# A retention loop with its score product one projection later and its value product one tile later, and its input loads a tile ahead

## The chip, the cores and the metric

The kernel runs on one core of one Trainium2 chip. A core has a matrix engine (TensorE, in the profile PE, with its weight loads as PEld) and three others that work beside it: VectorE (DVE), ScalarE (ACT) and GpSimd (POOL). SyncE (SP) issues most DMAs, and ACT a few. Each engine takes its own instructions in the order in which they stand in its queue. The metric is the device time of one execution, in microseconds (us); lower is better.

## The reference

One decoder layer on 2048 tokens of width 1024, in float32:

```python
h = x * (1.0 + scale_m) + shift_m                  # modulation from a conditioning vector
z = h @ w_in                                       # columns: 3 x 512 for a short convolution,
                                                   # 4 x 512 for q, k, v, g of 4 retention heads of 128
q = rotary(q); k = rotary(k) * 128 ** -0.5
# retention in chunks of 128 tokens (a "tile"), with a state carried from chunk to chunk
scores = einsum('bnihd,bnjhd->bhnij', qc, kc) * decay_mask
intra  = einsum('bhnij,bnjhe->bnihe', scores, vc)
inter  = einsum('bnihd,hi,nbhde->bnihe', qc, xi, prev_states)
y_ret  = silu(g) * head_groupnorm(intra + inter)
mix    = concat([y_conv, y_ret]) @ w_out
x = layernorm(alpha * x + gate_m * mix)
x = layernorm(alpha * x + gate_f * swiglu(x * (1 + scale_f) + shift_f))
```

## The kernel before

Each float32 matrix product is made of three float16 products (`mm3`, lines 135 to 137): both operands are split into a high and a low half (`split`, ACT at line 130 writes the high half, DVE at line 131 the low one). A program schedules the instructions of each engine from the written order, so some stand a little away from where they are written; the change section shows where they stand.

The stage of this case is a loop over the 128-token tiles t = 4 to 15 of the retention group. What one tile does:

- `gemm_ret(t, u)` for u = 0 to 3 projects the tile to k, q, v and g: 24 matmuls each into a PSUM bank, then one eviction, for u = 0 on DVE (L705), for u = 1 and 2 on ACT (L709), for u = 3 on ACT with silu (L711).
- `rotary(t)`: three DVE products (L734 to L736), then two POOL sums (L737, L738).
- `ret_transpose(t - 1)`: splits the rotated q and k of the tile before (ACT L130, DVE L131), sends each half through a transposing DMA on SP (L753), and lets POOL add the two halves of q (L756).
- `ret_scores(t - 1)`: 12 short float16 matmuls on the transposed q and k, evicted by DVE with the decay mask (L767).
- `ret_kv(t - 1)`: 4 float32 matmuls (L776) for the state; DVE adds (L782), POOL decays (L784).
- `ret_y(t - 1)`: 8 float32 matmuls (L793 with the scores, L796 with the state), then per-head statistics on DVE (L800, L802), the root on POOL (L804, L805), gate times root on POOL (L807), and the normalised product on DVE (L810). `ret_part` splits the result and frees the tile's pages; `ret_mix` stores it by a transposing DMA (L832).

Beside this the loop prepares later tiles. A pair of tiles shares one 256-token block of the input. `xt_load` brings a block from HBM (L231), `ret_h` modulates it on ACT (L296), `ret_hsplit` splits it, and `h_more` makes sums on POOL (L344 to L347), splits those too and stores all for the convolution (L356). In the tiles 7, 10, 11 and 13 an earlier block is loaded and treated again (`h_again`). The scale of all blocks from the fifth on comes from `h_scale()` in tile 6: DVE finds a bound (its last step is L291) and one small matmul (L99) spreads it over the partitions.

Memory is 24 pages of 8 KB per partition. `page(at)` takes a page from the list of free ones: with `at=0` the one freed longest ago, with `at=1` the next. A load into a page waits on SP until the last reader of that page is done, and everything behind it on SP waits too.

After the loop come the convolution group, the output projection with the first layer norm, the SwiGLU layer in two halves, and the second layer norm.

Of the kernel before, what the change touches and what calls it, by code (L numbers as in the profile page):

```python
# [24 lines left out]
NT = T // P  # L25
# [15 lines left out]
def kernel(ctx: ExitStack, tc: tile.TileContext, xT, x, c, adaN, adaT, ada_b, w_ret, w_conv,  # L41
# [187 lines left out]
    def xt_load(p, at=0):  # L229
        pg = page(at=at)  # L230
        nc.sync.dma_start(pg, xT[p])  # L231
        xt_pg[p] = pg
# [458 lines left out]
    def gemm_ret(t, u):  # L691
        hv, i4, _, ivh = hr[t // 2]
        if t not in qp:
            qp[t] = page(at=1)
        w_hi, w_lo = ret_w[u]
        ps = bank()
        for k in range(KT):
            mm3(ps, hv[:, t % 2, k // 4, 0, k % 4], hv[:, t % 2, k // 4, 1, k % 4], w_hi[:, k], w_lo[:, k],
                k == 0, k == KT - 1)
        dst = qp[t][:, u * 512:(u + 1) * 512]  # L700
        iv = i4[:, u:u + 1]
        if t % 2 == 0:
            nc.gpsimd.tensor_mul(iv, ivw[:, u:u + 1], ivh)
        if u == 0:
            nc.vector.scalar_tensor_tensor(  # L705
                dst.rearrange("p (h n) -> p h n", h=HEADS), ps.rearrange("p (h n) -> p h n", h=HEADS), iv,
                cst[:, 4:8][:, :, None].to_broadcast([P, HEADS, P]), op0=OP.mult, op1=OP.mult)
        elif u != 3:
            nc.scalar.activation(dst, ps, AF.Copy, scale=iv)  # L709
        else:  # L710
            nc.scalar.activation(dst, ps, AF.Silu, scale=iv)  # L711
# [46 lines left out]
    def ret_scores(t):  # L758
        tt = T1[t]
        th = tt.bitcast(F16)  # L760
        ps = aux()
        for h in range(HEADS):
            v = slice(h * P, (h + 1) * P)
            o = h * P
            mm3(ps[:, v], th[:, o:o + P], th[:, 1024 + o:1152 + o], th[:, 512 + o:640 + o], th[:, 1536 + o:1664 + o],
                True, True)
        nc.vector.scalar_tensor_tensor(tt[:, 1024:1536].rearrange("p (h n) -> p h n", h=HEADS),  # L767
                                       ps.rearrange("p (h n) -> p h n", h=HEADS), qk_s[t // 2][1],
                                       mask[:, None, :].to_broadcast([P, HEADS, P]), op0=OP.mult, op1=OP.mult)
# [47 lines left out]
    def ret_part(t):  # L817
        r = T1[t][:, 1536:2048]
        s = col(1, "s")
        row_scale(RM.pop(t), s, ivr[:, t:t + 1])  # L820
        rr = t2k(F16)
        split(r, rr[:, :512], rr[:, 512:1024], s)
        RR[t] = rr
        free(qp.pop(t), T1.pop(t))
# [35 lines left out]
    def cw_max(u):  # L860
        unit_max(cw_stage[u])
# [50 lines left out]
    def last_modulation():  # L912
        ada_bias(40, 48)
        row_of(mod[:, 5 * KT:6 * KT], gfrow, 1.0 / ALPHA)
# [160 lines left out]
    AGAIN = (7, 10, 11, 13)  # L1075
    for t in range(4, NT):
        p = t // 2 + 1
        if t % 2 == 0 and p < 8:
            xt_load(p, 1)
        end = t == NT - 1  # L1080
        ret_transpose(t - 1)
        gemm_ret(t, 0)
        if end:
            free(*ret_pages[0:2])
            cw_load(1)
            cw_max(0)
        if 4 < t < 13:
            ada_sum(t + 3)
        gemm_ret(t, 1)
        if 3 < t < 12:  # L1090
            ada_load(t + 4, -1)
        if end:
            free(*ret_pages[2:4])
            cw_split(0)
            cw_max(1)
            hp_load(0, 0)
            hp_load(0, 5)
        ret_scores(t - 1)
        ret_kv(t - 1)
        rotary(t)  # L1100
        if t == 4:
            ret_xmax(p)
        if t in (4, 5):
            for i in range(2):
                x_scan(2 * t - 4 + i)
        if t == 6:
            h_scale()
        if t in AGAIN:
            xt_load(AGAIN.index(t), 1)
        gemm_ret(t, 2)  # L1110
        if t > 4:
            ret_mix(t - 2)
        if end:
            free(ropep, *ret_pages[4:6])
            hp_load(0, 4)
            hp_load(0, 1)
            hp_load(0, 6)
        if t % 2 == 0 and p < 8:
            ret_h(p)
            ret_hsplit(p)  # L1120
        if t == NT - 2:
            cw_load(0)
        gemm_ret(t, 3)
        ret_y(t - 1)
        ret_part(t - 1)
        if end:
            free(*ret_pages[6:8])
            hp_load(0, 3)
            hp_load(0, 2)
        if t == 4:  # L1130
            ret_mix(2)
        if t in AGAIN:
            h_again(AGAIN.index(t))
        elif chores:
            chores.pop()()
        if t % 2 == 1:
            free(hr.pop(t // 2)[2])
# [31 lines left out]
    for b in range(2):  # L1169
        for u in range(6):  # L1170
            n = 6 * b + u
            if n == 5:
                for _ in range(3):
                    hp_load(1, ahead.pop(0))
            if n < 5:
                cw_split(u + 1)
                if u < 4:
                    cw_load(u + 2)
                    cw_max(u + 2)
            elif n < 11:  # L1180
                cw_again((u + 1) % 6)

            def done(m, b=b, u=u):
                if u == 5:
                    free(hp.pop((b, m)))
                    if b == 0 and ahead:
                        hp_load(1, ahead.pop(0))

            if 4 <= n < 8:
                ada_load(12 + n, -1)  # L1190
                ada_load(16 + n, -1)
            if 5 <= n < 9:
                ada_sum(11 + n)
                ada_sum_both(15 + n)
            if n == 3:
                mix_modulation()
            if n == 8:
                free(crow)
            if n == 9:
                more_modulation()  # L1200
            if n == 11:
                last_modulation()
            if n == 1:
                ret_scores(NT - 1)
                ret_mix(NT - 2)
            if n == 2:
                ret_y(NT - 1)
                free(spp)
            conv_pair(u, b, done)
            if n == 0:  # L1210
                ret_transpose(NT - 1)
            if n == 2:
                ret_part(NT - 1)
            if n == 3:
                ret_mix(NT - 1)
            if n == 6:
                conv_mix(0)
            if n == 7:
                wo_load(0)
            if n == 8:  # L1220
                wo_max(0)
                wo_split(0)
                wo_load(1)
            if n == 4:
                free(*cw_tmp)
            if n == 9:
                wo_max(1)
                wo_split(1)
                mixr_load(0)
            if n == 11:  # L1230
                mixr_load(2)
                mixr_load(1)
# [661 lines left out]
```

## Time and profile before

| | us |
|---|---|
| three runs | 2122.60, 2124.27, 2130.06 |
| median | 2124.27 |
| the profiled execution, device time | 2129.92 |
| its span in the trace | 2128.1 |
| PE busy | 2026.9 (95%) |
| DVE busy | 1461.7 (69%) |
| POOL busy | 953.9 (45%) |
| ACT busy | 666.7 (31%) |

The span lies 1.8 us below the device time of the same execution. PE is the engine that is busy nearly always, so a gain has to come out of the time in which it waits or runs at the lower of its two clocks. The core's mean granted clock was 0.987 of full speed.

### The profile page before, as it was taken

What the parts mean: (1) busy time and instruction counts of PE and PEld (TensorE: products, weight loads), DVE (VectorE), ACT (ScalarE), POOL (GpSimd) and SP (SyncE); (2) the same over time, 40 slices, a digit from 0 to 9 for tenths busy, and PEclk for the clock granted to TensorE, in tenths of its full rate; (3) what the DMA queues carried; (4) which work ended last, traced back from release to release, by engine and by line L of the source; (5) the groups of instructions that cost most, each with busy time, mean ns of one, the idle gap of its engine ahead of it and who ended that gap; (6) DMA issues with size and microseconds to landing.
All of it is one profiled execution on the core that took longest, in us unless ns stands there. A gap on an engine that the chain in (4) does not pass through costs nothing.

```text
span 2128.1 us, 24625 instructions
## 1 busy us (share of the span) xinstructions
PE 2026.9 (95%) x9631; PEld 949.7 (45%) x9631; DVE 1461.7 (69%) x1769; ACT 666.7 (31%) x728; POOL 953.9 (45%) x759
## 2 busy tenths in 40 slices
PE   8899898989899999799999999999999899999998
PEld 4355444444444544344444444444444344444443
DVE  7899556667677577768745677777767454378564
ACT  5522443424322222323323233333432122122210
POOL 3554655555742277733312344444447333134232
PEclk9999999999999999999999999999999999999999
DMA  9047454586684288765411234343345874475311
GB/s 375 25 136 237 129 159 109 150 263 190 219 315 168 82 236 200 176 180 205 149 50 60 98 131 144 126 141 134 135 167 203 298 309 175 157 271 189 149 71 78
DMA packets 189492, 361.06 MB, mean 170 GB/s; under 512 B 118080, under 2 KB 118080, under 8 KB 166592
## 3 DMA queue, kind: packets, MB, share of 16 engines
q1 hardware_dynamic: 181168, 344.55, 48.3%
q10 hardware_dynamic: 8208, 14.95, 2.0%
q8 instruction: 75, 1.23, 0.2%
q14 instruction: 41, 0.34, 0.0%
HBM read 231.26 MB, written 100.93 MB: 156 GB/s over the span
## 4 chain that ended last, share of the span: by engine, by line
PE 47%; DVE 5%; POOL 4%; DMA 4%; issue 2%; ACT 1%; SPq 0%; POOLq 0%; DVEq 0%; ACTq 0%
PE ax L135 8%; PE ax L136 8%; PE ax L137 8%; PE mm L135 8%; PE mm L136 8%; PE mm L137 8%; DMA pg<-in_w_dn_dram 1%; POOL pg L1612 1%; DMA pg<-yscr 1%; DMA yscr<-pg 1%; DVE wdm L87 1%; ACT pg L1272 1%; DVE pg L1611 1%; DVE pg L1335 1%; POOL pg L1336 1%
## 5 line engine op out<-in xcount | busy, mean ns | idle before, releaser
L135 PE MATMUL mm<-pg,pg 128*128 128x512 f16 x1604 | 608.6, 381 | 23.2 <-ACT pg L1420 8.2
L136 PE MATMUL mm<-pg,pg 128*128 128x512 f16 x1604 | 611.1, 381 | 0.0
L137 PE MATMUL mm<-pg,pg 128*128 128x512 f16 x1604 | 610.2, 381 | 0.5 <-DVE pg L889 0.5
L135 PE MATMUL ax<-pg,pg 128*128 128x512 f16 x1220 | 463.1, 380 | 12.4 <-DVE pg L1301 2.9
L136 PE MATMUL ax<-pg,pg 128*128 128x512 f16 x1220 | 463.2, 380 | 0.0
L137 PE MATMUL ax<-pg,pg 128*128 128x512 f16 x1220 | 461.6, 380 | 0.6 <-DVE pg L889 0.6
L135 PEld LDWEIGHTS <-pg 128*128 128x128 f16 x2888 | 284.1, 98 | 362.9 <-DMA pg<-pg 16.0
L136 PEld LDWEIGHTS <-pg 128*128 128x128 f16 x2888 | 284.1, 98 | 356.1 <-issue 30.4
L137 PEld LDWEIGHTS <-pg 128*128 128x128 f16 x2888 | 283.9, 98 | 350.3 <-issue 18.8
L1470 POOL TENSOR_TENSOR pg<-pg,t2k 128x512 f32<-128x512 f32 x44 | 57.9, 1317 | 328.6 <-DVE x L114 194.0
L131 DVE SCALAR_TENSOR_TENSOR pg<-pg,p2s,pg 128x2048 f16<-128x2048 f32 (+1 forms) x42 | 92.7, 2216 | 138.1 <-ACT pg L130 138.0
L130 ACT ACTIVATE pg<-pg,p2s 128x2048 f16<-128x2048 f32 (+1 forms) x42 | 77.5, 1858 | 262.3 <-PE mm L136 114.1
L1407 DVE TENSOR_TENSOR pg<-pg,pg 128x2048 f16<-128x2048 f32 x22 | 50.3, 2286 | 69.8 <-ACT pg L1406 69.8
L87 DVE TENSOR_REDUCE m<-pg 128x2 bf16<-128x2048 f32 (+1 forms) x38 | 86.3, 2276 | 16.2 <-DMA pg<-in_w_gu_dram 10.0
L525 PE MATMUL mm<-pg,pg 128*128 128x512 f16 x384 | 91.1, 393 | 5.6 <-DVE pg L533 2.5
L1475 ACT ACTIVATE pg<-t2k,ivg 128x512 f32<-128x512 f32 x44 | 31.5, 716 | 174.3 <-DVE t2k L1474 174.3
L1523 ACT ACTIVATE pg<-pg 128x2048 f16<-128x2048 f32 (+1 forms) x22 | 37.3, 1697 | 107.8 <-DMA wscr<-pg 69.6
L1524 DVE TENSOR_TENSOR pg<-pg,pg 128x2048 f16<-128x2048 f32 (+1 forms) x22 | 44.4, 2016 | 38.8 <-ACT pg L1523 38.8
L131 DVE SCALAR_TENSOR_TENSOR pg<-pg,hs,pg 128x1024 f16<-128x1024 f32 x32 | 48.5, 1535 | 29.2 <-ACT pg L130 29.0
L1264 POOL TENSOR_SCALAR rs<-mv 128x1 f32<-128x1 f32 x32 | 30.5, 957 | 82.2 <-DVE mv L1262 79.6
L1577 POOL TENSOR_TENSOR pg<-pg,pg 128x2048 f32<-128x2048 f32 (+1 forms) x6 | 26.9, 4490 | 82.0 <-DVE pg L131 38.6
L525 PEld LDWEIGHTS <-pg 128*128 128x128 f16 x384 | 38.0, 101 | 53.8 <-issue 10.0
(278 smaller groups left out, 2834.6 us busy)
## 6 DMA issues: line engine op xcount, KB each, us to landing
pg<-wscr SPq DMA_DIRECT2D x28, 1024.0 KB, 5.0
pg<-in_w_gu_dram SPq DMA_DIRECT2D x22, 1024.0 KB, 4.8
uscr<-pg SPq DMA_DIRECT2D x44, 512.0 KB, 2.7
pg<-in_w_dn_dram SPq DMA_DIRECT2D x22, 1024.0 KB, 5.8
pg<-in_adaT_dram SPq DMA_DIRECT2D x21, 1024.0 KB, 7.2
wscr<-pg SPq DMA_DIRECT2D x77, 256.0 KB, 2.9
yscr<-pg SPq DMA_DIRECT2D x16, 1024.0 KB, 4.9
pg<-uscr SPq DMA_DIRECT2D x16, 1024.0 KB, 6.5
```

The costliest lines, as they stand in the source:

```text
L87: return nc.vector.tensor_reduce(dst, src, axis=AX.X, op=OP.max, apply_absolute_value=True).ins
L130: nc.scalar.activation(hi, src, AF.Copy, scale=s)
L131: nc.vector.scalar_tensor_tensor(lo, src, s, hi, op0=OP.mult, op1=OP.subtract)
L135: nc.tensor.matmul(ps, l_hi, r_hi, start=start, stop=False, skip_group_check=again)
L136: nc.tensor.matmul(ps, l_hi, r_lo, start=False, stop=False, skip_group_check=again)
L137: return nc.tensor.matmul(ps, l_lo, r_hi, start=False, stop=stop, skip_group_check=again).ins
L525: nc.tensor.matmul(ps, hv[:, a, k, o], w[:, k], start=n == 0 and k == k0, stop=n == 2 and k == k1 - 1)
L1407: nc.vector.tensor_sub(wa[:, 2048:], pg, wa[:, :2048])
L1470: nc.gpsimd.tensor_add(e5, e5, p1)
L1475: nc.scalar.activation(u[:, 1], u2, AF.Silu, scale=iv_g)
L1523: nc.scalar.activation(o[:, :n, 0], src, AF.Copy)
L1524: nc.vector.tensor_sub(o[:, :n, 1], src, o[:, :n, 0])
```

## The change

Three edits, all in the loop over tiles and in the unit that follows it.

1. `ret_scores(t - 1)` and `ret_kv(t - 1)` are written after `gemm_ret(t, 2)` rather than after `gemm_ret(t, 1)`.
2. `ret_y` and `ret_part` of a tile are written after `gemm_ret(t, 0)` of the tile after the next, instead of at the end of the next tile: tile t now runs them for t - 2. The last of them goes to the start of the convolution.
3. `xt_load` is written one tile earlier, after `gemm_ret(t, 1)`, and takes the page that has been free the longest.

```diff
     for t in range(4, NT):
         p = t // 2 + 1
-        if t % 2 == 0 and p < 8:
+        if t == 4:
             xt_load(p, 1)
...
+        if t > 4:
+            ret_y(t - 2)
+            ret_part(t - 2)
         if 4 < t < 13:
             ada_sum(t + 3)
         gemm_ret(t, 1)
+        if t % 2 == 1 and p < 7:
+            xt_load(p + 1)
+        if t + 1 in AGAIN:
+            xt_load(AGAIN.index(t + 1))
...
-        ret_scores(t - 1)
-        ret_kv(t - 1)
         rotary(t)
...
-        if t in AGAIN:
-            xt_load(AGAIN.index(t), 1)
         gemm_ret(t, 2)
+        ret_scores(t - 1)
+        ret_kv(t - 1)
         if t > 4:
             ret_mix(t - 2)
...
         gemm_ret(t, 3)
-        ret_y(t - 1)
-        ret_part(t - 1)
...
+            if n == 0:
+                ret_y(NT - 2)
+                ret_part(NT - 2)
```

How the order on the engines moves. In the rows, the words behind the line are the operation and its operands; `pg` is a page, `ax` and `mm` are PSUM tiles, and numbers are buffers.

DVE in tile 9, before: L810 finishes the value product of tile 7, L705 evicts the first projection, L767 the scores of tile 8, then come the rotary products.

```order
L810 SCALAR_TENSOR_TENSOR pg_76<-ax_2250,mv_2260,pg_90 128x128 x4
L87 TENSOR_REDUCE g_2277<-pg_76 128x1
L705 SCALAR_TENSOR_TENSOR pg_91<-mm_2309,iv_1800,cst 128x512
L123 TENSOR_SCALAR g_2277<-g_2277 128x1
L125 TENSOR_SCALAR g_2277<-g_2277 128x1
L126 TENSOR_SCALAR s_2279<-g_2277 128x1
L131 SCALAR_TENSOR_TENSOR t2k_2284<-pg_76,s_2279,t2k_2284 128x512
L767 SCALAR_TENSOR_TENSOR pg_83<-ax_2364,pg_88,mask 128x512
L734 TENSOR_TENSOR pg_87<-pg_91,pg_86 128x1024
L735 TENSOR_TENSOR pg_87<-pg_91,pg_86 128x8x64
L736 TENSOR_TENSOR pg_87<-pg_91,pg_86 128x8x64
```

The same engine and tile now:

```order
L810 SCALAR_TENSOR_TENSOR pg_80<-ax_2298,mv_2308,pg_90 128x128 x4
L87 TENSOR_REDUCE g_2325<-pg_80 128x1
L123 TENSOR_SCALAR g_2325<-g_2325 128x1
L125 TENSOR_SCALAR g_2325<-g_2325 128x1
L734 TENSOR_TENSOR pg_87<-pg_97,pg_86 128x1024
L735 TENSOR_TENSOR pg_87<-pg_97,pg_86 128x8x64
L736 TENSOR_TENSOR pg_87<-pg_97,pg_86 128x8x64
L126 TENSOR_SCALAR s_2327<-g_2325 128x1
L131 SCALAR_TENSOR_TENSOR t2k_2332<-pg_80,s_2327,t2k_2332 128x512
L767 SCALAR_TENSOR_TENSOR pg_91<-ax_2397,pg_88,mask 128x512
L782 TENSOR_TENSOR t2k_2416<-ax_2411,pg_88 128x512
```

The rotary products stood behind the scores of the tile before, and now stand ahead of them.

PE in tile 6, before, at the small matmul of `h_scale` (L99): it stands inside the state product L776 that follows the second projection.

```order
L137 LDWEIGHTS pg_80
L137 MATMUL ax_1718<-pg_80 128x128
L776 MATMUL ax_1732<-pg_83 128x128
L99 LDWEIGHTS mh_1749
L99 MATMUL ax_1752<-ident_105,mh_1749 128x128
L776 MATMUL ax_1732<-pg_83 128x128 x3
```

And now, behind the value product of tile 4 (L793, L796), that is after the first projection of tile 6 and ahead of its second (L135):

```order
L796 MATMUL ax_1651<-pg_88,pg_78 128x128
L99 LDWEIGHTS mh_1728
L99 MATMUL ax_1731<-ident_105,mh_1728 128x128
L135 LDWEIGHTS pg_87
L135 MATMUL mm_1690<-pg_95,pg_87 128x512
```

It stands one projection and one score product earlier than before.

SP around the tiles 8 to 10, before: the transposes of tile 8 (L753), two input loads (L231), and the transposes of tile 9.

```order
L753 DMA_TRANSPOSE pg_83<-pg_98 128x8x128 x2
L832 DMA_TRANSPOSE pg_97<-t2k_2284 128x8x128
L231 DMA pg_76<-in_xT_dram 128x2048
L834 DMA mrscr_786<-pg_97 128x4096
L231 DMA pg_97<-in_xT_dram 128x2048
L753 DMA_TRANSPOSE pg_90<-pg_87 128x8x128 x2
```

And now:

```order
L231 DMA pg_78<-in_xT_dram 128x2048
L832 DMA_TRANSPOSE pg_98<-t2k_1914 128x8x128
L231 DMA pg_94<-in_xT_dram 128x2048
L832 DMA_TRANSPOSE pg_98<-t2k_2122 128x8x128
L753 DMA_TRANSPOSE pg_91<-pg_89 128x8x128 x2
L231 DMA pg_90<-in_xT_dram 128x2048
L832 DMA_TRANSPOSE pg_98<-t2k_2332 128x8x128
L834 DMA mrscr_786<-pg_98 128x4096
L753 DMA_TRANSPOSE pg_89<-pg_87 128x8x128 x2
```

The two loads moved from between the transposes of the tiles 8 and 9 to ahead of both, and the load of the tile after stands between them.

## Rows read from the trace of the kernel before

**Rows 1.** Windows, one tile each, 5 to 15: length, busy time by engine, clock, DMA.

```profile
162.53:186.65 24.12, 24.12 (x135) 12.87 (x132) 24.12 (x43) 6.80 (x9) 10.00 (x16) 1.00 0.88 257
186.65:213.46 26.81, 24.56 (x135) 13.01 (x133) 23.79 (x57) 8.62 (x17) 12.96 (x16) 1.00 0.71 226
...
244.93:270.86 25.93, 24.55 (x135) 12.81 (x132) 13.78 (x27) 13.62 (x20) 12.88 (x15) 1.00 0.38 104
...
296.57:327.89 31.32, 25.72 (x134) 13.69 (x132) 15.31 (x28) 17.06 (x27) 18.58 (x19) 0.97 0.52 174
...
sum 312.09, PE 279.16 PEld 148.49 DVE 209.57 ACT 117.56 POOL 170.35; mean PE 25.38 PEld 13.50 DVE 19.05 ACT 10.69 POOL 15.49
```

**Rows 2.** Waits of PE in tiles 6 to 15: total, times, longest (us).

```profile
PE ax L135 <- DMA pg<-pg: 15.2, 5, 4.8
PE ax L136 <- DMA pg<-pg: 12.6, 10, 1.8
PE ax L793 <- DVE pg L767: 3.6, 3, 2.6
```

**Rows 3.** Timeline of PE around tile 10: start, duration, instruction.

```profile
294.79 0.39 PE L793 MATMUL ax<-pg,pg 128*128 128x128 f32 x2
...
306.72 0.38 PE L137 MATMUL mm<-pg,pg 128*128 128x512 f16 x1
308.97 0.23 PE L135 MATMUL ax<-pg 128*128 128x128 f16 x1 [1.87 <-DMA pg<-pg]
```

**Rows 4.** Timeline of SP in tiles 9 to 11: start, time to issue.

```profile
294.98 0.46 SPq L231 DMA_DIRECT2D pg<-in_xT_dram  x1
...
305.75 2.62 SPq L753 DMA_TRANSPOSE pg<-pg  x2
...
335.57 1.28 SPq L753 DMA_TRANSPOSE pg<-pg  x1
```

**Rows 5.** Timeline of ACT in tile 10.

```profile
300.45 4.04 ACT L296 ACTIVATE pg<-pg,mod,msc 128x256 f32<-128x256 f32 x8 [7.12 <-DMA pg<-in_xT_dram]
304.40 1.31 ACT L130 ACTIVATE pg<-pg,pg 128x512 f16<-128x512 f32 x2
```

**Rows 6.** Timeline of POOL in tile 10.

```profile
310.40 1.15 POOL L756 TENSOR_TENSOR pg<-pg 128x512 f32<-128x512 f16 x1 [10.22 <-DMA pg<-pg]
...
318.06 1.03 POOL L807 TENSOR_TENSOR pg<-pg,rs 128x512 f32<-128x512 f32 x1
...
325.81 2.13 POOL L346 TENSOR_TENSOR pg<-pg 128x512 f32<-128x512 f32 x1
```

**Rows 7.** Timeline of DVE in tiles 9 and 10.

```profile
294.13 1.21 DVE L734 TENSOR_TENSOR pg<-pg,pg 128x1024 f32<-128x1024 f32 x1
295.26 0.68 DVE L735 TENSOR_TENSOR pg<-pg,pg 128x512 f32<-128x512 f32 x1
...
319.12 1.12 DVE L810 SCALAR_TENSOR_TENSOR pg<-ax,mv,pg 128x128 f32<-128x128 f32 x4 [3.22 <-POOL pg L807]
...
324.87 1.94 DVE L734 TENSOR_TENSOR pg<-pg,pg 128x1024 f32<-128x1024 f32 x1
326.73 1.75 DVE L735 TENSOR_TENSOR pg<-pg,pg 128x512 f32<-128x512 f32 x1
```

**Rows 8.** Timeline of DVE in tile 6.

```profile
199.20 0.67 DVE L291 TENSOR_TENSOR mh<-x,shm 128x1 bf16<-128x1 f32 x1
```

**Rows 9.** Waits of DVE in tiles 6 to 15.

```profile
DVE pg L131 <- ACT pg L130: 57.2, 21, 8.0
DVE pg L810 <- POOL pg L807: 25.3, 8, 7.1
```

**Rows 10.** Window of the convolution and the output projection.

```profile
475.00:905.00 430.00, 405.36 (x1916) 187.06 (x1915) 312.32 (x402) 137.29 (x140) 238.89 (x232) 0.99 0.64 200
```

**Rows 11.** Waits of SP in tiles 6 to 15.

```profile
SPq L832 <- DVE t2k L131: 44.6, 4, 16.9
...
SPq L231 <- DVE t2k L131: 22.1, 2, 11.1
```

## The prediction

> **What bounds the kernel now.** I first cut the loop into its tiles, from the first projection of one to that of the next [rows 1]. Tile 5 takes 24.12 us and PE is busy in all of it, so 24.12 us is what a tile costs when nothing waits. The eleven tiles from 5 to 15 take 312.09 us; at that floor they would take 11 x 24.12 = 265.3. So 46.8 us can be had in this loop, and tile 10 alone gives 7.2 of it. PE is busy for 279.16 of the 312.09 us. The missing 32.9 us are waits, and the 13.8 us by which 279.16 exceeds the floor are work at the lower of PE's two clock levels, 1.2 instead of 2.4 GHz: the granted clock of tile 10 is 0.97 of full speed on average, that of tiles 5 and 8 is 1.00 [rows 1]. A microsecond of waiting here thus comes with 13.8 / 32.9 = 0.42 us of slow work.
>
> The waits of PE say for what [rows 2]: 15.2 + 12.6 = 27.8 us are the first score matmuls waiting for a transposing DMA, and 3.6 us are value products waiting for the scores that DVE evicts. In tile 10 the last matmul of the second projection starts at 306.72, the first score matmul at 308.97, after a wait for the DMA [rows 3].
>
> Why the DMA is late shows in a chain over four engines. An input load leaves SP at 294.98 [rows 4]; ACT waits 7.12 us for it and modulates from 300.45, and only then, at 304.40, splits for the transposes of tile 9 [rows 5], which leave at 305.75 [rows 4]. POOL has waited 10.22 us for them at 310.40, and the gate times root of tile 8 (L807), which stands behind, runs at 318.06 [rows 6]. DVE has waited for that at 319.12; behind it in its queue stand the scores' eviction and then the rotary products, at 324.87 [rows 7]. The next transposes leave at 335.57 [rows 4], 29.8 us after the last: one late transpose makes the next late.
>
> **The change part by part.** Nothing is added or removed: PE, DVE, ACT, POOL and SP do the same instructions, and the DMAs are as many and as large. What counts is where they stand.
>
> *Scores a projection later.* A projection is 24 matmuls at (306.72 - 296.57) / 47 = 0.216 us, 5.18 us [rows 1, 3]. Ahead of the scores there now also stands a value product, 296.57 - 294.79 = 1.78 us [rows 1, 3]. The scores are wanted 6.96 us later in their tile. The longest waits for the two transposes are 4.8 and 1.8 us [rows 2], 6.6 together, so every wait is covered even if no transpose comes sooner. The cover is the third projection; without it the 27.8 us would stay. Bounds: 0 (the transposes slip by as much) and 27.8. I take 27.8, since DVE now has the rotary products ahead of the scores' eviction, and the circle of 29.8 us no longer passes through the scores.
>
> *Value product a tile later.* From the scores to it PE did the state product and the third and fourth projections; now it does the state product, the fourth and the next tile's first. The distance is the same, so I leave the 3.6 us [rows 2] and their slow work, 3.6 x 1.42 = 5.1 us (bounds: 0, and twice that). What stands behind on PE if it waits is the second projection and with it the rotary. Its POOL steps still stand behind the sum that waits for the transposes; that wait costs PE nothing until DVE's eviction of the scores comes too late for the next value product. The pages of a tile's projections and of its transposes are held a projection longer.
>
> *Input loads a tile earlier.* This removes no wait of PE by itself: ACT waits for them, with the split for the transposes behind. A load can leave only when its page is free. In the order now, the load into pg_90 stands on SP before the transposes of tile 9, and pg_90 is read by L810, the first of the DVE rows shown. So it still leaves near where it left, and ACT may wait some microseconds again. I cost this at nothing, because the 6.96 us covers it; without that cover it is 7.12 us in a tile with a load [rows 5].
>
> *The small matmul of the block scale (L99).* Here the change makes a wait. PE comes to it after the first projection and the value product of tile 6. Tile 6 began at 186.65 [rows 1], now 1.78 earlier, and 5.18 + 1.78 us later PE stands there: 191.8. Its operand was done at 199.20 + 0.67 = 199.87 [rows 8], and DVE was busy for all of tile 5 and 23.79 of the 26.81 us of tile 6 [rows 1], so it can't be much sooner. Bounds: 0 (the same work of DVE is reordered ahead of it in its favour) and 8.0. I take 4, which with the slow work is 5.7 us. Behind it on PE stand three projections of tile 6 and its scores, and the scale itself is what all later blocks wait for.
>
> *The convolution* gets one value product more at its start, which the loop gets less: nothing in the sum. Its order of instructions changes too, either way. It and the output projection have 430.00 - 405.36 = 24.6 us in which PE is not busy [rows 10]; I take no change, and a quarter of that, 6 us, as the bound on either side.
>
> **Sum.** 46.8 - 5.1 - 5.7 = 36.0 us. Against the profiled execution's own 2129.92 that is 2093.9. The median of the runs shown is 2124.27, 5.65 us below that execution, so I predict 2088.3.
>
> **The rivals.**
>
> *DVE sets the pace* (2101). It is busy for 209.57 / 11 = 19.05 us a tile [rows 1] and waits 57.2 + 25.3 = 82.5 us in the ten tiles from 6, for ACT and POOL [rows 9]. If the 25.3 us and half of the 57.2 stay, that is 5.4 us a tile. The rotary products take 1.21 + 2 x 0.68 = 2.57 us at 294.13, and 1.94 + 2 x 1.75 = 5.44 at 324.87 [rows 7], where POOL makes block sums, itself at 2.13 us [rows 6]. With closer tiles they meet more often: 2 us more a tile. Then ten tiles take 26.4 us and one 24.12, 288 in all, a gain of 24; with the whole 2.87 us, 27.3 a tile, 15. That gives 2101 to 2110. For it: tiles 5 and 6, where DVE is nearly full. Against: later tiles have DVE at 13.78 and 15.31 us of 25.93 and 31.32 [rows 1]. The Trainium skill has the mechanism in "SBUF — State Buffer", section "SBUF: two separate sides": VectorE and GpSimd share a port pair as an exclusive lock, and a VectorE instruction with two SBUF inputs blocks, or is blocked by, one of GpSimd that reads. The rotary rows agree with it, 1.75 us against 0.68.
>
> *The convolution gives it back* (2105). What DVE and POOL have not done when the loop ends is done in the convolution. If its idle time grows by half, 12.3 us, with the slow work 17.5, the gain falls to 18.5.
>
> *The transposes slip by as much as the scores do* (2124 to 2130). Then the change does nothing but make the wait at L99. For it: the circle above closes over POOL and the value product even now. Against: it would have to grow by 6.96 us, while the scores' eviction leaves it.
>
> *Slower: loads block the transposes on SP* (2173). The loop's eight loads stand in six places ahead of a pair of transposes, and SP waited up to 16.9 us for a store and 11.1 us for a page [rows 11]. If in each place a page held SP for 16.9 us, the scores would come 9.9 us beyond their cover: 6 x 9.9 x 1.42 = 85 us, 49 more than the gain. From 36 / (6 x 1.42) = 4.2 us beyond the cover, 11.2 us in each place, the kernel is slower than before. For it: pages are now held longer. Against: pg_90 is read by DVE ahead of the rotary products whose results the transposes carry, so the page is free first. The Trainium skill, "Perfetto Trace Analysis", section "Optimization Strategy", says that a gap that recurs on the engine that should be full can mean too little SBUF for the next tile. By that rule this change, which holds more pages, would be wrong; the rows of PE name a DMA between pages, not a buffer, so they don't bear it out.
>
> **How the numbers follow.** A measurement of this kernel can tell about 0.5%, 10.6 us, from no change. Chances: the forecast 0.52 (2078 to 2096: nothing at L99 and the convolution 6 better, to 8 us at L99); better than that 0.05; DVE's pace 0.22; the convolution 0.10; the slip 0.06; the block on SP 0.05. The range 2074 to 2110 holds the forecast, DVE's pace, most of the convolution's case and part of the better one. Faster by over 0.5% (under 2113.6) are the first four but for their worst ends, 0.86; within 0.5% the slip and those ends, 0.08; slower 0.06.
>
> **What would show it.** Right: tiles 7 to 15 near 24.1 to 24.6 us at clock 1.00, no wait of PE for a DMA at the scores, a wait of some 4 us at L99 in tile 6. DVE's pace: tiles near 26.4 us, PE waiting at L793 for L767. The slip: waits at the scores as before. The block: SP waiting at L231 with L753 behind it. The convolution: more idle PE behind the loop than 24.6 us. I am wrong if a tile waits at a place that none of these names.

## The result, and the profile after

| | before | after |
|---|---|---|
| median of the runs, us | 2124.51 (4 runs, 2122.60 to 2130.06) | 2113.76 (4 runs, 2111.77 to 2114.29) |
| the profiled execution | 2129.92 | 2113.66 |
| its span | 2128.1 | 2111.8 |

The ratio is 0.994, with a 95% interval from 0.9925 to 0.9954. The change is faster by 10.8 us; 36 were forecast, and 2113.76 lies above the range of 2074 to 2110.

The same tiles of the kernel after, 5 to 15, as windows (columns as in [rows 1]):

```profile
158.47:182.60 24.13, 24.13 (x134) 12.84 (x133) 23.11 (x45) 6.12 (x8) 10.28 (x15) 1.00 1.01 282
182.60:215.00 32.40, 26.67 (x135) 13.60 (x134) 26.55 (x63) 15.21 (x28) 15.56 (x20) 0.89 0.65 213
...
239.12:263.97 24.85, 24.38 (x134) 12.77 (x133) 19.17 (x35) 8.36 (x11) 19.83 (x19) 1.00 0.68 178
263.97:293.90 29.93, 26.07 (x134) 13.48 (x133) 16.23 (x33) 16.04 (x31) 12.23 (x11) 0.94 0.41 123
293.90:318.01 24.11, 24.11 (x134) 12.84 (x133) 9.15 (x16) 9.56 (x14) 15.99 (x16) 1.00 0.44 132
...
343.70:378.00 34.30, 28.01 (x134) 15.24 (x133) 21.62 (x27) 15.68 (x24) 21.21 (x15) 0.90 0.41 116
...
431.92:460.20 28.28, 26.43 (x151) 14.81 (x149) 19.16 (x49) 9.78 (x12) 17.00 (x16) 1.00 0.67 218
sum 301.73, PE 278.67 PEld 148.13 DVE 203.99 ACT 117.48 POOL 169.98; mean PE 25.33 PEld 13.47 DVE 18.54 ACT 10.68 POOL 15.45
```

Tiles 5 and 10 stand at the floor of 24.12 us, so the floor was real. Tiles 6, 9 and 12 take 32.40, 29.93 and 34.30. In all it is 301.73 us, 10.36 less than the 312.09 of [rows 1]. The two sums don't hold the same work: the last window now has a value product more (151 matmuls; it is that of tile 14, ahead of the convolution), 1.78 us, and tile 4 has one less. With the same work the loop became 12.1 us shorter: tiles 4 to 15 took 474.62 - 135.67 = 338.95 us before and 460.20 - 133.34 = 326.86 after, from the first projection of tile 4. The floor for the windows above is 265.3 + 1.78 = 267.1 us, and they stand 34.6 us above it: 23.06 us in which PE isn't busy, and 278.67 - 267.1 = 11.6 us of work at the lower clock.

The waits of PE in these tiles, as in [rows 2] (`L135 <- issue` is a wait at the scores of tile 12 for which the profile shows no releaser):

```profile
PE ax L793 <- DVE pg L767: 16.5, 6, 4.4
PE ax L99 <- DVE mh L291: 2.5, 1, 2.5
PE ax L135 <- issue: 1.3, 1, 1.3
PE ax L793 <- DVE g L125: 1.1, 1, 1.1
PE ax L793 <- DVE s L126: 0.7, 1, 0.7
PE ax L136 <- DMA pg<-pg: 0.7, 1, 0.7
```

The 27.8 us of waits at the scores [rows 2] have shrunk to 2.0. But the value products (L793) now wait 16.5 + 1.1 + 0.7 = 18.3 us, where they waited 3.6. The time left the scores and came back at the stage that uses them.

What a value product waits for shows in tile 9. First PE:

```profile
273.16 0.49 PE L793 MATMUL ax<-pg,pg 128*128 128x128 f32 x2 [3.86 <-DVE pg L767]
```

The score matmuls of the tile before had ended at 258.00. DVE evicted them 14.4 us later:

```profile
268.07 1.23 DVE L734 TENSOR_TENSOR pg<-pg,pg 128x1024 f32<-128x1024 f32 x1 [5.26 <-ACT pg L709]
269.21 0.68 DVE L735 TENSOR_TENSOR pg<-pg,pg 128x512 f32<-128x512 f32 x1
...
272.37 0.74 DVE L767 SCALAR_TENSOR_TENSOR pg<-ax,pg,mask 128x512 f32<-128x512 f32 x1
```

The eviction (L767) stands behind the rotary products, and the first of these waits 5.26 us for ACT to evict the second projection. ACT has that behind the modulation of a block, which waits for an input load:

```profile
263.42 4.04 ACT L296 ACTIVATE pg<-pg,mod,msc 128x256 f32<-128x256 f32 x8 [8.81 <-DMA pg<-in_xT_dram]
267.37 0.67 ACT L709 ACTIVATE pg<-mm,iv 128x512 f32<-128x512 f32 x1
```

In tile 12, where the value product waits 4.38 us at 353.40, L810 is ahead of the eviction as well:

```profile
340.61 1.13 DVE L810 SCALAR_TENSOR_TENSOR pg<-ax,mv,pg 128x128 f32<-128x128 f32 x4 [8.89 <-POOL pg L807]
...
347.47 1.22 DVE L734 TENSOR_TENSOR pg<-pg,pg 128x1024 f32<-128x1024 f32 x1
348.61 1.75 DVE L735 TENSOR_TENSOR pg<-pg,pg 128x512 f32<-128x512 f32 x1
...
352.61 0.74 DVE L767 SCALAR_TENSOR_TENSOR pg<-ax,pg,mask 128x512 f32<-128x512 f32 x1
```

The wait of 8.89 us is for the gate times root on POOL (L807), which stands behind the sum of the transposed halves (L756):

```profile
337.02 1.15 POOL L756 TENSOR_TENSOR pg<-pg 128x512 f32<-128x512 f16 x1 [10.75 <-DMA pg<-pg]
...
339.54 1.04 POOL L807 TENSOR_TENSOR pg<-pg,rs 128x512 f32<-128x512 f32 x1
```

So three things can hold the eviction: the rotary products ahead of it on DVE (theory A), ACT's modulation ahead of the second projection's eviction (B), and POOL's sum ahead of L807 (C). In tile 6, where the value product waits 3.22 us, there is a fourth: DVE is busy from 181.81 on without a wait, with the rotary products, L810 and the maxima of a block (L87, 4.48 us) ahead of the eviction at 190.35. In tile 12 L735 takes 1.75 us against 0.68 in tile 9, while POOL makes a block sum (L344, 347.64 to 349.81). This agrees with what the Trainium skill, "SBUF — State Buffer", section "SBUF: two separate sides", says of a port pair that these two engines share. L734, which started 0.17 us before that sum, took 1.22 unstretched. The same section of the Trainium skill has it that the one that starts first keeps the ports. This makes one wait longer and isn't why the eviction stands last.

### The profile page after: what moved, and what is told of

Same layout as the page of the kernel before. It is cut to its first block, busy times and chain, and to the rows that moved or that the text cites. A ratio compares the mean times of both kernels' runs of the same rounds, so it can differ in the third digit from the quotient of the medians.

```text
span 2111.8 us, 24628 instructions
## 1 busy us (share of the span) xinstructions
PE 2023.6 (96%) x9631; PEld 947.1 (45%) x9631; DVE 1448.7 (69%) x1769; ACT 666.9 (32%) x728; POOL 946.0 (45%) x759
## 4 chain that ended last, share of the span: by engine, by line
PE 46%; DVE 7%; POOL 4%; DMA 4%; issue 2%; ACT 1%; SPq 0%; POOLq 0%; DVEq 0%; ACTq 0%
PE mm L135 8%; PE mm L136 8%; PE mm L137 8%; PE ax L135 8%; PE ax L136 8%; PE ax L137 8%; DMA pg<-in_w_dn_dram 1%; ACT pg L1278 1%; DVE wdm L87 1%; DVE pg L1341 1%; POOL pg L1342 1%; DMA pg<-yscr 1%; POOL rs L1270 1%; DVE st L1267 1%; DVE pg L1307 1%
## 5 line engine op out<-in xcount | busy, mean ns | idle before, releaser
L135 PE MATMUL mm<-pg,pg 128*128 128x512 f16 x1604 | 609.5, 382 | 22.6 <-ACT pg L1426 8.2
L135 PE MATMUL ax<-pg,pg 128*128 128x512 f16 x1220 | 463.6, 380 | 9.7 <-DVE t2k L973 4.3
L136 PEld LDWEIGHTS <-pg 128*128 128x128 f16 x2888 | 283.5, 98 | 354.5 <-issue 28.0
L135 PEld LDWEIGHTS <-pg 128*128 128x128 f16 x2888 | 283.4, 98 | 347.2 <-issue 10.9
L137 PEld LDWEIGHTS <-pg 128*128 128x128 f16 x2888 | 283.4, 98 | 342.5 <-issue 7.1
L87 DVE TENSOR_REDUCE m<-pg 128x2 bf16<-128x2048 f32 (+1 forms) x38 | 86.3, 2275 | 18.1 <-DMA pg<-in_w_conv_dram 10.0
L1482 DVE SCALAR_TENSOR_TENSOR pg<-pg,ivg,pg 128x512 f32<-128x512 f32 x44 | 60.8, 1382 | 1.1
```

Of the source, the lines that this page charges most:

```text
L87: return nc.vector.tensor_reduce(dst, src, axis=AX.X, op=OP.max, apply_absolute_value=True).ins
L135: nc.tensor.matmul(ps, l_hi, r_hi, start=start, stop=False, skip_group_check=again)
L136: nc.tensor.matmul(ps, l_hi, r_lo, start=False, stop=False, skip_group_check=again)
L137: return nc.tensor.matmul(ps, l_lo, r_hi, start=False, stop=stop, skip_group_check=again).ins
L1482: nc.vector.scalar_tensor_tensor(u[:, 1], e5, iv_u, u[:, 1], op0=OP.mult, op1=OP.mult)
```

## Experiments

Times are medians; each ratio is to the kernel before, in runs on the same chip. Differences between two changed kernels are of medians from different chips; by the ratios they come out the same within 2 us. In the diffs `behind(i, j)` keeps instruction i after j in the order of their engine, with no wait of its own. Every kernel is scheduled anew, so an edit for one engine can move some instructions on the others; where that bears on a reading, the text says so.

### The parts alone, the distance, and POOL's sum

**The third edit alone**, on the kernel before:

```diff
-        if t % 2 == 0 and p < 8:
+        if t == 4:
             xt_load(p, 1)
...
+        if t % 2 == 1 and p < 7:
+            xt_load(p + 1)
+        if t + 1 in AGAIN:
+            xt_load(AGAIN.index(t + 1))
...
-        if t in AGAIN:
-            xt_load(AGAIN.index(t), 1)
```

> The kernel before with edit 3 alone (input loads a tile earlier), scores and value product where they were. Theory (the gain is the scores' later place): the scores still wait for their transposes, some 28 us in the loop, and the time is 2118 to 2128 us. Rival (the earlier loads make the gain, since the split for the transposes no longer waits for the modulation): the waits of PE for the transposes fall under 10 us and the time is 2100 to 2114 us.

2121.94 us, ratio 0.9986 (0.9977 to 0.9995), with 20.6 us of waits at the scores, less than the theory's 28 and more than the rival's 10. **The first and second edit alone** (the diff of the change without these lines):

> The changed kernel with its loads where they were before (edits 1 and 2 alone). Theory (the loads do nothing much): PE waits at the value product for the evicted scores as in the changed kernel, 16 us or more, and the time is 2108 to 2120 us. Rival (loads a tile earlier hold pages and block SP or ACT, and so cost what the later scores gain): under 2105 us, with ACT waiting less than 39.5 us for the input.

2124.68 us, ratio 0.9993 (0.9981 to 1.0004), outside both ranges. The waits of PE of this kernel, from 155 to 475 us (this stretch in all the fences of waits below; in the faster kernels its end lies in the convolution):

```profile
PE ax L793 <- DVE pg L767: 14.8, 4, 5.9
PE ax L99 <- DVE mh L291: 4.8, 1, 4.8
PE mm L135 <- DVE pg L705: 4.6, 1, 4.6
```

With no wait for a transpose, and the value products waiting, these two edits give nothing. The third gives 2 to 3 us alone and 10.9 on top of the others: the parts don't add up, which a sum of separate terms can't say.

**More distance.** The value product of the changed kernel one projection later still:

```diff
-        if t > 4:
-            ret_y(t - 2)
-            ret_part(t - 2)
         if 4 < t < 13:
             ada_sum(t + 3)
         gemm_ret(t, 1)
+        if t > 4:
+            ret_y(t - 2)
+            ret_part(t - 2)
```

> The changed kernel with the value product one projection later again (after the second projection rather than the first), 5.18 us more between scores and value product. Theory (DVE evicts the scores late by an order of waits, by at most 4.4 us beyond what PE allows): the 18 us of waits at the value product vanish and with them their slow work, 18 x 1.42 = 26 us: 2086 to 2096 us. Rival (DVE has too much work for a shorter tile): the eviction slips by as much and the time stays at 2108 to 2118 us.

2128.50 us, ratio 1.0008 (0.9998 to 1.0019), above both ranges:

```profile
PE mm L135 <- ACT pg L709: 10.1, 2, 9.6
PE ax L793 <- DVE pg L767: 7.3, 3, 3.5
PE ax L99 <- DVE e L116: 5.9, 1, 5.9
```

The value products' wait falls from 16.5 to 7.3, but projections now wait for their PSUM banks, which ACT evicts late. Distance alone is no cure; the theory that it was all that lacked fell here.

**POOL's sum behind the next rotary sums:**

```diff
-        if t > 0:
+        if 0 < t < 4:
             nc.gpsimd.tensor_add(T1[t][:, 1536:2048], dst[:, 512:1024], dst[:, 1536:2048])
...
+        if t > 4:
+            ret_qsum(t - 1, last)
```

> The changed kernel with POOL's sum of the transposed halves (L756) held behind the rotary sums of the next tile, so that POOL's gate of the value product no longer stands behind a wait for the transposes. Theory (that wait, 32.7 us on POOL, is what holds L810 and behind it the scores' eviction on DVE): DVE's wait for the gate falls from 33.2 to under 15 us, PE's waits at the value product from 18 to under 9, and the time is 2095 to 2106 us. Rival (DVE is full, or waits for ACT anyway): 2108 to 2118 us.

2110.32 us, ratio 0.9923 (0.9905 to 0.994), in the rival's range. In this file lines behind 738 have moved by nine, so L802 is the product with the scores, L805 that with the state, L776 the eviction and L745 the sum:

```profile
PE ax L802 <- DVE pg L776: 10.2, 4, 4.4
PE ax L805 <- POOL pg L745: 9.7, 4, 5.5
```

The wait for the eviction fell by 6 us, and a wait for the sum itself took its place.

### What holds the eviction

**The order on DVE turned round in the kernel before:** the eviction behind the rotary products.

```diff
+        c = nc.vector.tensor_mul(b4[:, :, 1], q4[:, :, 0], sinb); rot_ins[t] = (a.ins, b.ins, c.ins)
...
+        [behind(ev.ins, i) for i in rot_ins.get(t + 1, ())]
...
+        rotary(t)
         ret_scores(t - 1)
         ret_kv(t - 1)
-        rotary(t)
```

> The kernel before, with the order on DVE turned round: the eviction of the scores (L767) stands behind the rotary products (L734 to L736) of the tile instead of ahead of them. Nothing is left out. There six value products start 0.8 to 2.8 us after the eviction, so an eviction 2.5 us later is waited for. Theory A: the value products' waits grow from 3.6 to some 10 to 15 us, and nothing pays for it but rotary products 0.7 us sooner: 2128 to 2140. If the order on DVE doesn't matter, since ACT and POOL set when the rotary and the eviction come: 2121 to 2127.

2130.49 us, ratio 1.002 (1.0011 to 1.0028).

```profile
PE ax L793 <- DVE pg L767: 23.6, 9, 5.5
...
PE ax L135 <- DMA pg<-pg: 2.0, 1, 2.0
PE ax L136 <- DMA pg<-pg: 1.2, 2, 0.8
```

This is the clearest run. Through the loop PE runs the same instructions in the same order as before, and yet the waits at the scores fall from 27.8 us [rows 2] to 3.2, while those at the value products rise from 3.6 to 23.6. On ACT a few evictions (L709, L711) and on POOL some state decays (L784) and sums (L756) moved past a neighbour with it; what the edit orders is DVE. That order turns the one wait into the other. The first edit brought the same order by its place in the program, and its later scores got the credit in the forecast.

**The eviction ahead of the rotary products, in the changed kernel:**

```diff
-        rotary(t)
...
         gemm_ret(t, 2)
-        ret_scores(t - 1)
+        rotary(t, ret_scores(t - 1))
         ret_kv(t - 1)
```

with `[behind(i.ins, e) for e in ev for i in (a, b, c)]` in `rotary`.

> The changed kernel, with one thing moved on DVE: in the tiles from 4 on the rotary products (L734 to L736) stand behind the eviction of the scores (L767) instead of ahead of it. Nothing is left out. In the changed kernel eight value products wait, 19.7 us in all, and in each of them the eviction comes 3.4 to 8.5 us after the first rotary product, more than the wait. Theory A (the rotary products stand ahead of the eviction on DVE, and they wait for an eviction of ACT): the eviction comes sooner by these 3.4 to 8.5 us, the 19.7 us go, with the slow work behind them some 28; some of it comes back at the scores, since the rotary is later: 2086 to 2100. Theory C (POOL's sum of the transposed halves holds the gate times root, and with it DVE's L810, which stands ahead of the eviction in either order): only the waits in which L810 was early go: 2103 to 2112.

2105.76 us, ratio 0.9905 (0.989 to 0.992), 8.0 us less than the changed kernel and in the range of theory C.

```profile
PE ax L793 <- DVE pg L767: 6.9, 2, 4.2
PE ax L135 <- DMA pg<-pg: 3.5, 1, 3.5
...
PE ax L136 <- DMA pg<-pg: 1.9, 2, 1.6
```

Of eight waits (18.3 us; the expectation has 19.7) two are left. In one of them DVE still has L810 ahead of the eviction, waiting for POOL:

```profile
238.89 1.12 DVE L810 SCALAR_TENSOR_TENSOR pg<-ax,mv,pg 128x128 f32<-128x128 f32 x4 [3.38 <-POOL pg L807]
...
241.13 0.74 DVE L767 SCALAR_TENSOR_TENSOR pg<-ax,pg,mask 128x512 f32<-128x512 f32 x1
```

Both theories had a part: A was right on the place, C on what was still ahead. In the loop PE keeps its order but for L99. Yet the run isn't DVE's order alone: ACT was scheduled otherwise, too, and in tile 11 the eviction of the second projection (L709, 333.31) now stands ahead of the block's modulation (L296, 336.47), where in the changed kernel it stood behind (346.14 and 341.15).

**The modulation on ACT behind the third projection's eviction:**

```diff
-            nc.scalar.activation(src[:, k], src[:, k], AF.Identity, scale=msc[:, 0, k:k + 1], bias=mod[:, k:k + 1])
+            x = nc.scalar.activation(src[:, k], src[:, k], AF.Identity, scale=msc[:, 0, k:k + 1], bias=mod[:, k:k + 1]).ins; [behind(x, j) for j in last[-1:]]
...
-            nc.scalar.activation(dst, ps, AF.Copy, scale=iv)
+            last.append(nc.scalar.activation(dst, ps, AF.Copy, scale=iv).ins)
```

> The changed kernel, with the modulation of a block (L296) put on ACT behind the eviction of the third projection of the tile in which it is written; ACT then waits for an input load only when the evictions of the second and third projection are done. Nothing is left out. Theory B (ACT's wait for the input load, 39.5 us in six places, holds the eviction of the second projection, for which DVE's rotary products and behind them the scores' eviction wait): the value products' waits in tiles 6, 8 and 11, 11.9 us, go, 17 with the slow work: 2095 to 2104. Theory C (POOL): 2108 to 2115. If the later modulation makes the convolution's stores or the next block late: 2116 or more.

2113.14 us, ratio 0.9937 (0.9923 to 0.9951), no different from the changed kernel.

```profile
PE ax L135 <- DMA pg<-pg: 9.7, 2, 5.6
PE ax L793 <- DVE pg L767: 6.3, 2, 3.8
...
PE ax L136 <- DMA pg<-pg: 1.0, 1, 1.0
```

The value products wait 12.0 us less (18.3 to 6.3) and the scores 8.7 us more (2.0 to 10.7). B is right on the value products' wait and the kernel wins nothing: an exchange once more. Why the transposes come late here isn't shown. Ahead of the first wait (355.94) ACT's split stood behind 7.96 us of modulation, but it was done at 326.04 and the transposes left SP only at 351.30; ahead of the second (382.06) the split waited for POOL's rotary sums (L738). PE was scheduled otherwise as well: the scores of the first wait stand 114 matmuls of projections behind the value product, where the changed kernel has 48. So this run doesn't show what ACT's order is worth by itself.

**Without POOL's sum:**

```diff
-        if t > 0:
+        if 0 < t < 4:
             nc.gpsimd.tensor_add(T1[t][:, 1536:2048], dst[:, 512:1024], dst[:, 1536:2048])
...
-                nc.tensor.matmul(ps[:, v], tt[:, 1536 + h * P:1536 + (h + 1) * P], S[t][:, v], start=False, stop=True)
+                nc.tensor.matmul(ps[:, v], tt[:, 1536 + h * P:1536 + (h + 1) * P] if t < 4 else mask, S[t][:, v], start=False, stop=True)
```

> The changed kernel without POOL's sum of the transposed halves of q (L756) from tile 4 on; the state product reads a constant table in its place, so this part of the computation is left out. Everything else is issued as before. Theory C (the sum waits on POOL for the transposes, 32.7 us in seven places, and holds L807 behind it, for which DVE waits 33.2 us in nine places with the scores' eviction behind): DVE's 33.2 us fall to under 10, the value products' waits in tiles 11, 12, 14 and 15 (10.8 us) go: 2094 to 2103. Theory A (the order on DVE alone): the waits at L810 fall but the eviction still stands behind the rotary, which waits for ACT: 2106 to 2113.

2104.43 us, ratio 0.9896 (0.9881 to 0.9912): 9.3 us less than the changed kernel, between the two ranges. The kernel leaves the sum out, so the time is that of a program with less work on POOL.

```profile
PE ax L793 <- DVE pg L767: 8.8, 5, 3.7
```

L767 is the releaser of 8.8 us still, with the rotary ahead of it; two more value products wait 4.4 us, so 13.2 of the 18.3 us are left.

### The eviction first, and what is left

**The eviction ahead of L810 as well,** on top of the kernel with the eviction ahead of the rotary products: `ret_y` returns its last DVE steps as a function.

```diff
-        for h in range(HEADS):
+        def finish(ev=()):
+            for h in range(HEADS):
...
+                                           op0=OP.subtract, op1=OP.mult); [behind(i.ins, e) for e in ev]
...
-            ret_y(t - 2)
-            ret_part(t - 2)
+            fin = ret_y(t - 2)
...
-        rotary(t, ret_scores(t - 1))
+        ev = ret_scores(t - 1); rotary(t, ev)
...
-            ret_mix(t - 2)
+            fin(ev); ret_part(t - 2); ret_mix(t - 2)
```

> The kernel with the eviction of the scores ahead of the rotary products (2105.8 us), and the last DVE step of the value product of the tile before (L810, its maximum and the split behind it) put behind that eviction too. Nothing is left out. Two value products still wait there, 7.4 us in all, and ahead of the eviction in these tiles stand L810, which waits for POOL's L807, and block splits (L131) that wait for ACT. If L810 holds the eviction: both go, 7 to 11 us with the slow work, 2095 to 2099. If the block splits hold it as well: 2102 to 2107.

2097.55 us (2094.50 to 2099.52), ratio 0.9867 (0.9854 to 0.9881): 16.2 us less than the changed kernel, the best version here.

```profile
PE ax L136 <- DMA pg<-pg: 5.3, 2, 3.0
PE mm L135 <- DMA pg<-hcscr: 4.1, 1, 4.1
PE mm L135 <- ACT pg L709: 3.5, 1, 3.5
...
PE ax L135 <- issue: 1.5, 1, 1.5
PE ax L793 <- DVE pg L767: 0.9, 1, 0.9
```

The second line is a wait for a load of the convolution, until 455.76, behind the loop.

In the changed kernel DVE came to the eviction late; now it stands ready before the scores do in four tiles, 16.1 us in all, and the wait has the other direction. One of the four:

```profile
303.78 0.75 DVE L767 SCALAR_TENSOR_TENSOR pg<-ax,pg,mask 128x512 f32<-128x512 f32 x1 [6.12 <-PE ax L137]
```

**The sum on DVE,** right ahead of the eviction, with the eviction ahead of the rotary products:

```diff
+        ps = aux(); sm = [nc.vector.tensor_add(tt[:, 1536:2048], th[:, 512:1024], th[:, 1536:2048]).ins] if t > 3 else []
...
+        [behind(ev.ins, i) for i in sm]; return [ev.ins]
```

> The kernel of the run before with the eviction of the scores ahead of the rotary products (2105.8 us), and POOL's sum of the transposed halves of q (L756) now made by DVE, right ahead of that eviction, from tile 4 on. Nothing is left out. Moving the eviction alone gave 8.0 us, leaving the sum out alone gave 9.3 us. If these are two separate holds on the eviction (the rotary products ahead of it; L810 ahead of it, which waits for L807, which stands behind the sum on POOL), the gains add, less some 0.7 us a tile of DVE work that is mostly hidden: 2094 to 2100. If both take away the same waits: 2103 to 2108.

2108.14 us, ratio 0.9918 (0.9905 to 0.9932). Together with the edit above it:

> Both edits of the two runs beside it: eviction of the scores ahead of the rotary products and of L810, and the sum of the transposed halves on DVE. Nothing is left out. If what is left of the value products' waits comes from L810 and L807 alone, no value product waits, and the tiles stand at the floor but for the scores' waits and the wait at L99: 2086 to 2096. If something else holds the eviction (block splits waiting for ACT, DVE's own work): 2098 to 2106.

2099.40 us, ratio 0.988 (0.9867 to 0.9894). Neither is better than the kernel without the sum on DVE (2105.76 and 2097.55). The gains of the order (8.0) and of the sum's absence (9.3) don't add. Part of that may be that both take away the same wait of the eviction, part that DVE now waits for the transposes where POOL did, 23.5 us in eight places in the first of the two. These runs don't part the two.

**The third edit undone,** with the eviction ahead of the rotary products (the first diff under "Experiments", backwards):

> The kernel with the eviction of the scores ahead of the rotary products (2105.8 us), with the input loads where the kernel before has them (the third edit undone). Nothing is left out. With the eviction behind the rotary products, undoing the loads cost 10.9 us (2124.7 against 2113.8). If the earlier loads pay since the rotary products, and behind them the eviction, wait for ACT, which waits for a load: with the eviction in front they pay little, 2105 to 2110. If they pay by the splits for the transposes, which stand behind the modulation on ACT in either order: 2113 to 2118.

2118.52 us, ratio 0.9966 (0.9954 to 0.9979): 12.8 us more than with the loads a tile earlier.

```profile
PE ax L135 <- DMA pg<-pg: 7.9, 4, 3.1
PE ax L136 <- DMA pg<-pg: 5.8, 6, 1.9
```

With the loads where they were, the waits at the scores come back, 13.7 us, though the scores stand a projection later. So with the eviction in front the earlier loads pay by the splits for the transposes, and the 6.96 us did not cover them. In the changed kernel it is otherwise: with the loads undone there no wait for a transpose shows, but 4.8 us at L99 and 4.6 at a projection that waits for DVE (L705).

**Are the deeper stages needed?** The third edit and the order on DVE alone, on the kernel before, with `ret_y` as in the kernel with the eviction ahead of L810, and L810 behind the eviction and the rotary products:

```diff
-        ret_scores(t - 1)
+        ev = ret_scores(t - 1)
         ret_kv(t - 1)
-        rotary(t)
+        ev += rotary(t); [(fin(ev), ret_part(t - 2)) for i in range(t > 4)]
...
-        ret_y(t - 1)
-        ret_part(t - 1)
+        fin = ret_y(t - 1)
+        if end: fin(); ret_part(t - 1)
```

> The kernel before with the third edit alone (input loads a tile earlier, 2121.9 us) and the order on DVE of the best version: the last DVE step of the value product (L810) and what follows it stand behind the scores' eviction and the rotary products of the next tile. Scores and value product stand on PE where the kernel before has them. Nothing is left out. If the order on DVE and the loads are what costs, and the deeper stages aren't needed: 2096 to 2103, near the best version's 2097.6. If the scores a projection later are needed, the first score matmuls wait for the transposes as in the kernel before (20.6 us with the third edit alone) and the time stays: 2112 to 2122.

2108.06 us, ratio 0.9909 (0.9891 to 0.9927), between the two expectations.

```profile
PE ax L135 <- issue: 6.1, 1, 6.1
PE ax L135 <- DMA pg<-pg: 6.0, 1, 6.0
PE ax L136 <- DMA pg<-pg: 4.8, 3, 2.7
```

All three lines are waits at the scores, 16.9 us. **The later scores without the later value product,** on the best version:

```diff
-            fin = ret_y(t - 2)
...
-        gemm_ret(t, 3)
+        gemm_ret(t, 3); fin = ret_y(t - 1) if not end else ret_y(t - 1)()
```

> The best version (2097.6 us) with the second edit undone: the value product stands at the end of the next tile again, one projection behind the scores instead of two. Nothing is left out. In the best version the scores' eviction comes 5.3 to 10.2 us behind the scores in seven of the loop's tiles, and one projection with the state product is some 6.1 us: if the distance counts, four value products wait some 4 us each, 20 to 25 us with the slow work: 2112 to 2123. If the eviction comes late only since nothing waits for it: 2096 to 2102.

2104.37 us, ratio 0.9899 (0.9882 to 0.9916), just above the second range.

```profile
PE ax L136 <- DMA pg<-pg: 7.2, 2, 4.0
PE ax L793 <- DVE pg L767: 3.8, 2, 3.2
```

Order and loads without either deeper stage give some 19 us, more than the whole change; later scores bring 3.7 more, which at these spreads is hardly more than nothing, and the later value product another 6.8. The value products wait 3.8 us, not the four waits of 4 us that distance would give: the eviction comes late mostly when nothing waits for it.

## Why the prediction was wrong

**The step that failed** is in the change part by part: "DVE now has the rotary products ahead of the scores' eviction, and the circle of 29.8 us no longer passes through the scores", with "The distance is the same, so I leave the 3.6 us" behind it. The circle did leave the scores, and closed through the value product, which needs the eviction. The upper bound was twice 3.6 us; 18.3 were measured. Each microsecond of wait came with 11.6 / 23.06 = 0.50 us of slow work (0.42 forecast), so this term is 18.3 x 1.50 = 27.5 us instead of 5.1, and the 22.4 us between them are nearly the whole gap in the loop: forecast 36.0, measured 12.1. Shown by the order turned round (the waits change places with PE's order untouched) and by the order put right (0.9 us left, 16.2 us won). The forecast had even named the condition, that DVE's eviction "comes too late for the next value product", and left it without a price. The sentence on the order that I used for the gain was the one that priced the loss.

**Scores a projection later.** As a forecast of the waits at the scores it held: 27.8 us to 2.0. As a cause it did not: the turned order does that without it, and with the loads undone and the eviction in front 13.7 us are back behind the same cover. The 2.0 us are in part luck. In tile 12 the transposes left 20.2 us into the tile (9.9 before):

```profile
363.91 3.66 SPq L753 DMA_TRANSPOSE pg<-pg  x2
```

At the floor the scores are wanted 17.3 us into a tile, as in tile 10; here PE came to them only at 367.3, 23.6 us in, since its value product had waited first. In the best version, where it doesn't wait, the scores wait 6.8 us (5.3 and 1.5).

**The loads at nothing.** They are worth 2 to 3 us alone, 10.9 with the other edits and 12.8 with the eviction in front. The reason given for nothing, that the 6.96 us covers ACT's wait, fell with the eviction in front; why they are worth 10.9 us with it behind, where no transpose is waited for, was not followed up beyond the waits at L99 and L705.

**L99.** Forecast 4 us of wait, from 191.8 on PE; measured 2.51, up to 196.12. Right in kind, and in size by luck: a value product just ahead had already waited 3.22 us. Without that PE would have come to L99 at about 187.77 + 1.78 = 189.6 and waited some 6.5 us (an estimate).

**The convolution.** Behind the loop the rest took 2128.1 - 474.62 = 1653.5 us before and 2111.8 - 460.20 = 1651.6 after: no change, within the bound of 6.

**The base.** The profiled execution before stood 5.4 us above the median, that after 0.1 below, so the profiles differ by 16.3 us and the medians by 10.8. The 16.3 are 2.3 us ahead of the loop (tile 4 begins at 135.67 before and 133.34 after), where the change touches nothing, 12.1 in the loop and 1.9 behind it. The forecast took 5.65 us off the base and left the gain of 36.0, read from that one execution, whole; how much of the 5.65 lay in its loop isn't known.

**The rivals.** DVE's pace gave the right sign (PE waiting at L793 for L767, tiles of some 27 us on average), but, except in tile 6, not by its mechanism: DVE is busy for 203.99 of 301.73 us, less than before, and another order of the same work wins 16.2. The slip came in single tiles, as in tile 12 above, and was hidden there; the block on SP did not show: SP's waits at L231 fell from 35.8 to 14.6 us.

What stays open: of the 9 us between the best version and the forecast of 2088.3, its waits name 6.8 us at the scores, 3.5 at a late eviction of ACT and, behind the loop, 4.1 at a load of the convolution; these were not tried one by one. The order on DVE without the earlier loads and without the deeper stages was not run either. Nor was it followed up why projections wait for ACT where the value product is moved a projection further.

## What to carry to other kernels

Where engines wait for each other in a circle, a wait that disappears at one consumer has to be looked for at the next consumer of the same queue. Before a stage is moved, read what will stand ahead of its eviction on the in-order engine, and when that will be ready; the number of matmuls between producer and consumer says little if the eviction is queued behind something that waits for a DMA. Try the order on the queue first: here, with the earlier loads, it gave some 19 us, more than the deeper pipeline with the same loads (10.8).

## What was not expected of the hardware

The price of a wait in slow work is not constant. Tile 12 lost 34.30 - 28.01 = 6.29 us to waits and 28.01 - 24.12 = 3.89 to the lower clock (0.90 on average), tile 8 lost 0.47 and 0.26 at a mean clock of 1.00. Before, tile 10 lost 5.60 to waits and 1.60 to the clock (0.97) [rows 1]. Over the eleven tiles it is 0.42 us for each microsecond of wait before and 0.50 after. What sets it isn't shown here.
